# Earlier operand products and splits by DMA at the entry of a ConvFFN, on one core

## The chip, the cores and the metric

The kernel runs on one core of a Trainium2 chip. The metric is the device time of one execution in microseconds; lower is better. A core has the engines TensorE (PE in the profile, with its weight loads as PEld), VectorE (DVE), ScalarE (ACT), GpSimd (POOL) and SyncE (SP, which in this kernel issues the DMAs).

## The reference, cut to what matters

One decoder layer on 1024 tokens of 1024 channels, in float32: three token mixers, a merge, and then a pre-norm gated MLP with a causal convolution of width 3. The change lies where this MLP begins:

```python
x = x + merged @ w_o[l]

h = _rmsnorm(x, g_ffn[l])
u = _causal_dwconv(h @ w_up[l], ff_conv_w[l], ff_conv_b[l])
u_val, u_gate = jnp.split(u, 2, axis=-1)
x = x + (jax.nn.silu(u_gate) * u_val) @ w_down[l]
```

## The kernel before

Everything is held transposed: channels on the 128 partitions, tokens (reversed) along a row of 1024, in two halves of 512. A matrix product in float32 precision is made of three matmuls in the faster float32r format (`mm3`, lines 149 to 151). For this each operand is split in two: `hi` is the operand rounded to float32r, `lo` the rest. `split` writes `hi` on ACT (line 136) and `lo = src - hi` on DVE (line 137). Line 149 multiplies hi by hi, line 150 the weight's hi by the activation's lo, line 151 the weight's lo by the activation's hi. In the profile's names the tile after the arrow that comes first is the activation's part, the second the weight's (`whi`, `wlo`; both names serve for hi and lo of weights, since one tile holds both parts side by side).

Products with `w_up` go by a Strassen-Winograd scheme of seven half-size products. `seven` (from line 671) is a generator that makes one unit, that is two 128-column blocks of `w_up`, in four steps: step 1 the products with the operands `au` and `bu`, step 2 those with `t2` and `t3`, step 3 that with `t1`, step 4 those with `bl` and `t4`. For a unit it loads two weight tiles `r1` and `r2`, and DVE forms sums of their halves: `s1` (line 693), `a2 - ...` into the half `a2` (694), and `a1` for T2 (695). PSUM results are copied out by ACT (lines 689, 699, 704, 709) and added by DVE (691, 705, 712). Units 0, 1 and 2 (`first` in the code) are interleaved by hand at the entry. Their weight tiles are, by buffer number, raw_1423 and pg_1424 (unit 0), raw_1431 and pg_1432 (unit 1), me_1439, me_1440 and pg_1441 (unit 2).

The operands are linear combinations of the normalised halves. `bau` and `bbu` hold the upper half, ready before. At the entry, once `rows` is there (1/rms of the lower half's tokens, a PSUM tile ps_tr_1422 made by line 179), DVE forms the others for j = 0 and 1, each 128 x 1024: `diff[j]` (h_1301, h_1302) times `rows` is the source of t3; `full[j]` (pg_1289, pg_1290) plus `diff[j]` that of t2 (lines 1142 to 1148); `x1p[2+j]` (px_1351, px_1352) times gain and `rows` is bl, and bl minus `full[j]` is the source of t1, in `x1p[j]` (y_1349, y_1350; lines 1151 to 1157); `full[2+j]` (pg_1291, pg_1292) minus `full[j]` is that of t4 (lines 1160 to 1163). Their hi and lo parts are h_1398 to h_1401 (t2), pg_1402 to pg_1405 (t3), h_1406 to h_1409 (t1), pg_1410 to pg_1413 (bl) and h_1414 to h_1417 (t4); the lo parts have the odd numbers.

What sets the order: the code is traced as written, and a scheduler then gives each engine a fixed order by priority (the place in the code) and by what it estimates to be ready. `tc.high_priority(offset=n)` moves the instructions in its block forward in priority by n. Weight splits in `qring` have an offset of 40 (`SOON`). Each engine runs its own order strictly one after the other and waits at semaphores. DMAs are issued from SP's queue in its order; POOL issues none.

Of the kernel before, what the change touches and what calls it, by code (L numbers as in the profile page):

```python
# [10 lines left out]
F32 = mybir.dt.float32  # L11
F32R = mybir.dt.float32r
AF = mybir.ActivationFunctionType
ALU = mybir.AluOpType
# [28 lines left out]
def tile_hybrid_layer(ctx: ExitStack, tc: tile.TileContext, xT, memT, vecs, w_t, w_n, w_kv, w_if,  # L43
# [4 lines left out]
    nc = tc.nc  # L48
# [19 lines left out]
    def T(shape, tag, dt=F32, bufs=None):  # L68
        pool = {"mw": mlp, "mst": mlp, "px": late[0]}.get(tag, sb)
        return pool.tile(shape, dt, tag=tag, name=nm(tag), bufs=bufs or BUFS[tag])  # L70

    def page(tag="pg", dt=F32):
        return T([P, S], tag, dt)
# [4 lines left out]
    def wide():  # L78
        return T([P, S], "U")
# [22 lines left out]
    def hs(h):  # L102
        return slice(h * HALF, (h + 1) * HALF)
# [25 lines left out]
    def col(i, n=1):  # L129
        return vec[:, i:i + n]  # L130
# [4 lines left out]
    def split(src, hi, lo, eng=None):  # L135
        nc.scalar.activation(hi, src, AF.Copy)  # L136
        (eng or nc.vector).tensor_sub(lo, src, hi.bitcast(F32))  # L137

    def wsplit(src, tag=None, eng=None, raw=None):
        if raw is None:  # L140
            raw = T([P, S], "raw")
            nc.sync.dma_start(raw, src)
        hi = T([P, S], tag or "whi", F32R)
        lo = T([P, S], tag or "wlo", F32R)
        split(raw, hi, lo, eng)
        return hi, lo
# [21 lines left out]
    def rstd_rows(acc, n):  # L168

        return spread(rstd(acc, n), n // P)  # L170
# [111 lines left out]
    def x_norm(h, xp, rows):  # L282
        for j in range(4):
            t = wide()
            for k in (2 * j, 2 * j + 1):
                u = t[:, hs(k % 2)]
                nc.vector.scalar_tensor_tensor(u, xp[j][:, hs(k % 2)], col(C_GMIX + k), rows, op0=ALU.mult, op1=ALU.mult)  # L287
                split(u, hh[k][:, hs(h)], hl[k][:, hs(h)])
            nc.sync.dma_start(hn_d[h, j], t)
# [16 lines left out]
    for g in range(2):  # L306
        src = wraw[:, :, 4 * g:4 * g + 4]
        hi = wif[:, :, 32 * g:32 * g + 4]
# [352 lines left out]
    def qring(src):  # L661
        t = pair(turn(0, ("whi", "wlo")))
        with tc.high_priority(offset=SOON):
            split(src, *t)
        return t
# [399 lines left out]
    full = [page() for _ in range(4)]  # L1065
# [8 lines left out]
    diff = [page("h") for _ in range(2)]  # L1074
    for h in (1, 0):
        x1s = []
        acc = half()
        x1p = [wide() if h else T([P, S], ("y", "px")[i // 2]) for i in range(4)]
# [21 lines left out]
        for d in range(KT):  # L1100
            proj(w_o[d], m_hi, m_lo, ev(d), halves=(h,))
            if h == 0 and d > 0:
                if d == 1:
                    rows = rstd_rows(kept[0], HALF)
# [29 lines left out]
    fd, fx = {}, {"au": bau, "bu": bbu}  # L1134
# [3 lines left out]
    rows = rstd_rows(kept[0], HALF)  # L1138
    first = units[:3]
    for u in first:  # L1140
        next(u)
    for j in range(2):
        for i in range(2):
            nc.vector.tensor_mul(diff[j][:, hs(i)], diff[j][:, hs(i)], rows)
        nc.vector.tensor_add(full[j], full[j], diff[j])
        split(full[j], *fd["t2"][j])
    for j in range(2):
        split(diff[j], *fd["t3"][j])
    for u in first[:2]:
        next(u)  # L1150
    for j in range(2):
        bl = x1p[2 + j]
        for i in range(2):
            nc.vector.scalar_tensor_tensor(bl[:, hs(i)], bl[:, hs(i)], col(C_GFFN + 4 + 2 * j + i), rows,
                                           op0=ALU.mult, op1=ALU.mult)
        nc.vector.tensor_sub(x1p[j], bl, full[j])
        split(x1p[j], *fd["t1"][j])
    for u in first[:2]:
        next(u)
    for j in range(2):  # L1160
        split(x1p[2 + j], *fd["bl"][j])
        nc.vector.tensor_sub(full[2 + j], full[2 + j], full[j])
        split(full[2 + j], *fd["t4"][j])
    next(first[0])
    middle(first[2])
    next(first[1])
# [74 lines left out]
    au, al, bu, bl, wc = [], [], [], [], []  # L1241
# [167 lines left out]
```

## Time and profile before

| | us |
|---|---|
| three runs | 1677.52, 1679.14, 1679.28 (median 1679.14) |
| the profiled execution | 1682.24, span of the profile 1680.5 |
| PE busy | 1650.0 (98%) |
| DVE busy | 1209.4 (72%) |
| ACT busy | 825.4 (49%) |
| POOL busy | 51.7 (3%) |

All durations come from the one profiled execution; it took 3.1 us longer than the median of the three timed runs. The mean granted TensorE clock over it is 0.998 of full speed. The ConvFFN entry lies at 1040 to 1090 us of the span: line 1144 runs on DVE from 1046.4 to 1053.7, line 1154 from 1060.6, line 1156 from 1064.0, line 1162 from 1075.2. A row of a timeline gives start, length, engine, line, operation, out<-in and count, and in brackets how long the engine had been idle and who ended that. Rows of a DVE or ACT timeline overlap a little, since a length runs to the last write; how much an instruction holds its engine is read from one start to the next.

### The profile page before, as it was taken

The page shows a single profiled execution, that of the slowest core. Times are in us where ns is not written, and L with a number is a line of the kernel's source. Part 1 is how long each engine was busy: PE and PEld are TensorE (multiplying, and loading weights), DVE is VectorE, ACT ScalarE, POOL GpSimd, SP SyncE. Part 2 cuts the span into 40 slices and gives each one's busy share as a digit, 9 for nine tenths or more (in the row PEclk, how much of TensorE's full clock was granted, in tenths as well). Part 3 has the DMA queues.
Part 4 walks back from the last instruction along what each step waited for, and adds up shares of the span by engine and source line. Part 5 has one row for each costly group of instructions (what it writes and reads, how often), then busy time and mean ns, then how long its engine had stood idle before and what let it go on. Part 6 is the DMA issues. An engine that isn't in the chain of part 4 may idle for free.

```text
span 1680.5 us, 21196 instructions
## 1 busy us (share of the span) xinstructions
PE 1650.0 (98%) x7975; PEld 1340.4 (80%) x7975; DVE 1209.4 (72%) x1710; ACT 825.4 (49%) x1249; POOL 51.7 (3%) x95
## 2 busy tenths in 40 slices
PE   8999999999999999999999999999999999999999
PEld 4777777787777888888778888688888888788887
DVE  5648777777954766766457648997778877789864
ACT  4547677645544445656312334565555554543431
POOL 1000000010000101000000000000000000000000
PEclk9999999999999999999999999999999999999999
DMA  8421011233334564422856354222222221486142
GB/s 294 148 64 33 26 39 51 98 122 114 122 117 150 189 185 151 142 101 102 283 180 192 108 190 149 83 93 100 88 76 75 76 89 62 163 325 238 33 139 74
DMA packets 96249, 212.69 MB, mean 127 GB/s; under 512 B 12416, under 2 KB 36224, under 8 KB 96148
## 3 DMA queue, kind: packets, MB, share of 16 engines
q1 hardware_dynamic: 96148, 211.35, 37.0%
q8 instruction: 63, 1.03, 0.3%
q14 instruction: 38, 0.31, 0.1%
HBM read 156.71 MB, written 54.61 MB: 126 GB/s over the span
## 4 chain that ended last, share of the span: by engine, by line
PE 88%; DVE 4%; ACT 4%; DMA 3%; issue 1%; SPq 0%; POOLq 0%; ACTq 0%; DVEq 0%
PE ps_pj L149 14%; PE ps_pj L150 14%; PE ps_pj L151 14%; PE ps_pv L150 6%; PE ps_pv L149 6%; PE ps_pv L151 6%; PE ps_tr L149 4%; PE ps_tr L151 4%; PE ps_tr L150 4%; PE ps_z L149 3%; PE ps_z L150 3%; PE ps_z L151 2%; PE ps_tr L434 2%; PE ps_pv L448 1%; PE ps_z L226 1%
## 5 line engine op out<-in xcount | busy, mean ns | idle before, releaser
L150 PE MATMUL ps_pj<-h,whi 128*128 128x512 f32 x620 | 242.5, 391 | 0.0
L136 ACT ACTIVATE whi<-raw 128x512 fp32r<-128x512 f32 (+1 forms) x112 | 93.6, 836 | 181.1 <-PE ps_pj L150 75.8
L149 PE MATMUL ps_pj<-h,whi 128*128 128x512 f32 x412 | 163.3, 396 | 1.3 <-DVE U L1052 1.2
L149 PE MATMUL ps_pj<-pg,whi 128*128 128x512 f32 x396 | 155.4, 393 | 0.7 <-ACT U L699 0.7
L151 PE MATMUL ps_pj<-pg,wlo 128*128 128x512 f32 x380 | 148.2, 390 | 0.2 <-DVE wlo L137 0.2
L150 PEld LDWEIGHTS ps_pj<-h,whi 128*128 128x128 f32 x620 | 116.5, 188 | 23.6 <-DVE U L287 0.2
L151 PE MATMUL ps_pj<-h,wlo 128*128 128x512 f32 x332 | 130.1, 392 | 0.7 <-DVE wlo L137 0.7
L810 DVE SCALAR_TENSOR_TENSOR y<-U,vec,y 128x1023 f32<-128x1023 f32 x88 | 112.4, 1279 | 8.0 <-ACT y L808 8.0
L422 DVE TENSOR_TENSOR_SCAN U<-U 128x512 f32<-128x512 f32 (+3 forms) x96 | 88.6, 965 | 30.6 <-ACT U L415 29.7
L149 PEld LDWEIGHTS ps_pj<-h,whi 128*128 128x128 f32 x412 | 77.5, 188 | 18.6 <-ACT whi L136 1.6
L137 DVE TENSOR_TENSOR wlo<-raw,whi 128x1024 fp32r<-128x1024 f32 x54 | 66.0, 1222 | 33.4 <-ACT whi L136 33.4
L149 PEld LDWEIGHTS ps_pj<-pg,whi 128*128 128x128 f32 x396 | 74.5, 188 | 16.9 <-ACT U L699 1.6
L151 PEld LDWEIGHTS ps_pj<-pg,wlo 128*128 128x128 f32 x380 | 71.4, 188 | 15.5 <-DVE wlo L137 0.6
L136 ACT ACTIVATE whi<-pg 128x512 fp32r<-128x512 f32 (+1 forms) x59 | 43.4, 738 | 73.5 <-PE ps_pv L150 20.3
L151 PEld LDWEIGHTS ps_pj<-h,wlo 128*128 128x128 f32 x332 | 62.4, 188 | 14.3 <-DVE wlo L137 1.6
L150 PE MATMUL ps_pj<-pg,whi 128*128 128x512 f32 x188 | 73.7, 392 | 0.0
L150 PE MATMUL ps_pv<-h,whi 128*128 128x512 f32 x164 | 63.9, 390 | 0.0
L808 ACT ACTIVATE y<-U,vec 128x1024 f32<-128x1024 f32 x44 | 54.6, 1241 | 15.2 <-DVE U L712 15.2
L151 PE MATMUL ps_pj<-h,whi 128*128 128x512 f32 x156 | 60.9, 390 | 0.0
L151 PE MATMUL ps_tr<-pg,wlo 128*128 128x512 f32 x144 | 56.2, 390 | 0.3 <-DVE wlo L137 0.3
L137 DVE TENSOR_TENSOR whi<-raw,whi 128x512 fp32r<-128x512 f32 x58 | 39.9, 688 | 23.0 <-ACT whi L136 22.7
L436 ACT ACTIVATE y<-ps_tr 128x1024 f32<-128x1024 f32 (+3 forms) x48 | 39.1, 814 | 31.6 <-PE ps_tr L434 31.2
(438 smaller groups left out, 4314.3 us busy)
## 6 DMA issues: line engine op xcount, KB each, us to landing
raw<-in_w_t_dram SPq DMA_DIRECT2D x29, 512.0 KB, 3.8
gate_d<-U SPq DMA_DIRECT2D x24, 512.0 KB, 3.0
U<-gate_d SPq DMA_DIRECT2D x24, 512.0 KB, 3.9
pg<-in_w_up_dram SPq DMA_DIRECT2D x22, 512.0 KB, 3.9
act_d<-y SPq DMA_DIRECT2D x22, 512.0 KB
pg<-in_w_t_dram SPq DMA_DIRECT2D x21, 512.0 KB, 4.6
raw<-in_w_dn_dram SPq DMA_DIRECT2D x18, 512.0 KB, 3.4
raw<-in_w_o_dram SPq DMA_DIRECT2D x16, 512.0 KB, 3.4
```

Source lines behind the costliest of these rows:

```text
L136: nc.scalar.activation(hi, src, AF.Copy)
L137: (eng or nc.vector).tensor_sub(lo, src, hi.bitcast(F32))
L149: nc.tensor.matmul(out, lh, rh, start=start, stop=False, skip_group_check=more)
L150: nc.tensor.matmul(out, lh, rl, start=False, stop=False, skip_group_check=more)
L151: nc.tensor.matmul(out, ll, rh, start=False, stop=stop, skip_group_check=more)
L226: nc.tensor.matmul(pm[m], mg[k // 4][:, c], w[:, hs(kk)], start=(k == 0), stop=(k == KT - 1))
L422: nc.vector.tensor_tensor_scan(f[:, a, 1:w + 1], f[:, a, 1:w + 1], f[:, a, 1:w + 1], 1.0 if o == 0 else f[:, a, 0:1], op0=ALU.mult, op1=AL ...
L434: nc.tensor.transpose(pt[:, a, ts(j)], g[:, a, ts(j)], ident)
L436: nc.scalar.activation(wt[:, :, :w], pt[:, :, :w], AF.Copy)
L448: nc.tensor.matmul(pv[64 * a:64 * a + 64, ts(rb % 4)], sbv[s // 2][:, s % 2, (2 * p + a) * 64:(2 * p + a + 1) * 64], wt[:, a, ts(j)], star ...
L808: nc.scalar.activation(out, u, AF.Identity, bias=bias, scale=taps[0])
L810: nc.vector.scalar_tensor_tensor(out[:, :S - s], u[:, s:], taps[s], out[:, :S - s], op0=ALU.mult, op1=ALU.add)
```

## The change

A new helper, `split_add`, writes `hi` on ACT, then `-hi` on ACT into the tile of `lo`, and then adds the source to it by a DMA that GpSimd issues. It is used for the six tiles of t1, bl and t4. The lines that form t2 and t3, with their splits, get a priority offset of 200.

```diff
+    def split_add(src, hi, lo):
+
+        nc.scalar.activation(hi, src, AF.Copy)
+        nc.scalar.activation(lo, hi.bitcast(F32), AF.Copy, scale=-1.0)
+        nc.gpsimd.dma_start(lo, src, accum_op=ALU.add)
...
-    for j in range(2):
-        for i in range(2):
-            nc.vector.tensor_mul(diff[j][:, hs(i)], diff[j][:, hs(i)], rows)
-        nc.vector.tensor_add(full[j], full[j], diff[j])
-        split(full[j], *fd["t2"][j])
-    for j in range(2):
-        split(diff[j], *fd["t3"][j])
+    with tc.high_priority(offset=200):
+        for j in range(2):
+            for i in range(2):
+                nc.vector.tensor_mul(diff[j][:, hs(i)], diff[j][:, hs(i)], rows)
+            nc.vector.tensor_add(full[j], full[j], diff[j])
+            split(full[j], *fd["t2"][j])
+        for j in range(2):
+            split(diff[j], *fd["t3"][j])
...
-        split(x1p[j], *fd["t1"][j])
+        split_add(x1p[j], *fd["t1"][j])
...
-        split(x1p[2 + j], *fd["bl"][j])
+        split_add(x1p[2 + j], *fd["bl"][j])
         nc.vector.tensor_sub(full[2 + j], full[2 + j], full[j])
-        split(full[2 + j], *fd["t4"][j])
+        split_add(full[2 + j], *fd["t4"][j])
```

Lines behind the helper move down by six, and those behind the new block by seven (L695 becomes L701, L704 becomes L710, L1154 becomes L1161).

The order on DVE right behind the first two L693 rows (units 0 and 1), before:

```order
L694 TENSOR_TENSOR pg_1424_8632<-raw_1423_8630,pg_1424_8632 128x512
L694 TENSOR_TENSOR pg_1432_8675<-raw_1431_8673,pg_1432_8675 128x512
L695 TENSOR_TENSOR raw_1423_8630<-hf_1430_8669,raw_1423_8630 128x512
L695 TENSOR_TENSOR raw_1431_8673<-hf_1438_8712,raw_1431_8673 128x512
L693 TENSOR_TENSOR hf_1447_8757<-pg_1441_8720 128x512
L1144 TENSOR_TENSOR h_1301_7943<-h_1301_7943,ps_tr_1422_8628 128x512
```

and in the changed kernel, where the first of these rows stands too, from the row behind it (the L1151 rows are L1144 of before, L1152 is L1145, L700 and L701 are L694 and L695):

```order
L1151 TENSOR_TENSOR h_1301_7943<-h_1301_7943,ps_tr_1422_8628 128x512 x2
L1151 TENSOR_TENSOR h_1302_7944<-h_1302_7944,ps_tr_1422_8628 128x512
L1152 TENSOR_TENSOR pg_1289_7931<-pg_1289_7931,h_1301_7943 128x1024
L1151 TENSOR_TENSOR h_1302_7944<-h_1302_7944,ps_tr_1422_8628 128x512
L137 TENSOR_TENSOR pg_1403_8599<-h_1301_7943,pg_1402_8598 128x1024
L137 TENSOR_TENSOR h_1399_8595<-pg_1289_7931,h_1398_8594 128x1024
L1152 TENSOR_TENSOR pg_1290_7932<-pg_1290_7932,h_1302_7944 128x1024
L137 TENSOR_TENSOR pg_1405_8601<-h_1302_7944,pg_1404_8600 128x1024
L137 TENSOR_TENSOR wlo_1444_8724<-me_1439_8716,wlo_1444_8724 128x512
L137 TENSOR_TENSOR h_1401_8597<-pg_1290_7932,h_1400_8596 128x1024
L697 TENSOR_TENSOR U_1428_8651<-U_1428_8651,ps_z_1426_8635 128x512
L701 TENSOR_TENSOR raw_1423_8630<-hf_1430_8669,raw_1423_8630 128x512
```

The ten rows that form and split t2 and t3 now stand ahead of the sum that makes raw_1423, the T2 weight of unit 0.

The order on ACT from the hi part of t1, before (U_1449 and U_1453 are results of units 0 and 1 copied from PSUM):

```order
L136 ACTIVATE h_1406_8602<-y_1349_8246 128x1024
L136 ACTIVATE h_1408_8604<-y_1350_8247 128x1024
L689 ACTIVATE U_1445_8739<-ps_tr_1442_8722 128x512
L699 ACTIVATE U_1449_8790<-ps_tr_1425_8634 128x512
L136 ACTIVATE wlo_1456_8851<-hf_1430_8669 128x512
L699 ACTIVATE U_1453_8823<-ps_pj_1433_8677 128x512
L136 ACTIVATE wlo_1458_8897<-raw_1423_8630 128x512
L704 ACTIVATE U_1449_8790<-ps_tr_1425_8634 128x512
```

and in the changed kernel, from the row before the second hi part (L142 writes -hi, L695, L705 and L710 are L689, L699 and L704 of before):

```order
L142 ACTIVATE h_1407_8603<-h_1406_8602 128x1024
L141 ACTIVATE h_1408_8604<-y_1350_8247 128x1024
L695 ACTIVATE U_1445_8739<-ps_tr_1442_8722 128x512
L705 ACTIVATE U_1449_8790<-ps_tr_1425_8634 128x512
L705 ACTIVATE U_1453_8823<-ps_pj_1433_8677 128x512
L142 ACTIVATE h_1409_8605<-h_1408_8604 128x1024
L136 ACTIVATE wlo_1458_8903<-raw_1423_8630 128x512
L136 ACTIVATE whi_1460_8923<-pg_1424_8632 128x512
L142 ACTIVATE pg_1411_8607<-pg_1410_8606 128x1024
L141 ACTIVATE h_1414_8610<-pg_1291_7933 128x1024
L141 ACTIVATE pg_1412_8608<-px_1352_8249 128x1024
L142 ACTIVATE h_1415_8611<-h_1414_8610 128x1024
```

The next two rows there are `L710 ACTIVATE U_1449` and then the pass that writes -hi of the second bl tile, pg_1413: the new passes stand between and behind copies that wait for PE.

POOL's queue had no DMA; in the changed kernel it ends with these six, in this order:

```order
L143 DMA h_1407_8603<-y_1349_8246 128x1024
L143 DMA h_1409_8605<-y_1350_8247 128x1024
L143 DMA pg_1411_8607<-px_1351_8248 128x1024
L143 DMA h_1415_8611<-pg_1291_7933 128x1024
L143 DMA pg_1413_8609<-px_1352_8249 128x1024
L143 DMA h_1417_8613<-pg_1292_7934 128x1024
```

Each waits for ACT's -hi pass of its tile, and the matmuls of line 150 with that tile (L156 now) wait for its landing.

On PE, the 60 matmuls from the first with t3 or t2 (number 4179 in its order) to the last ahead of t1 (4238) are the same set in another order; those with t1, bl and t4 (from 4239) keep their place within a few rows.

## The prediction

> **What bounds the kernel now.** I read the page's head first, then the chain that ended last, then a table of stretches around the changed place, and last the timeline of each engine there.
>
> ```profile
> span 1680.5 us, 21196 instructions
> ...
> PE 1650.0 (98%) x7975; PEld 1340.4 (80%) x7975; DVE 1209.4 (72%) x1710; ACT 825.4 (49%) x1249; POOL 51.7 (3%) x95
> ...
> PE 88%; DVE 4%; ACT 4%; DMA 3%; issue 1%; SPq 0%; POOLq 0%; ACTq 0%; DVEq 0%
> ```
>
> TensorE (PE) is the bound: any microsecond that it stands still is a microsecond of the span, and work taken off VectorE (DVE) or ScalarE (ACT) is worth something only where PE waits for it. So the question is how long PE waits at the ConvFFN entry now. The table of stretches (length, busy time by engine, granted clock, DMA share, GB/s) answers that:
>
> ```profile
> core 0: us, PE busy (x) PEld busy (x) DVE busy (x) ACT busy (x) POOL busy (x), PEclk, DMA share, GB/s
> ...
> 1052.00:1056.00 4.00, 1.71 (x5) 0.93 (x5) 4.00 (x6) 3.58 (x4) 0.00 (x0) 0.94 0.00 0
> 1056.00:1060.00 4.00, 4.00 (x13) 3.12 (x13) 4.00 (x5) 1.06 (x1) 0.00 (x0) 0.63 0.00 0
> 1060.00:1064.00 4.00, 4.00 (x19) 3.34 (x18) 2.57 (x5) 1.28 (x2) 0.00 (x0) 1.00 0.00 0
> 1064.00:1071.00 7.00, 6.74 (x28) 4.74 (x27) 7.00 (x10) 3.96 (x6) 0.00 (x0) 1.00 0.00 0
> 1071.00:1073.00 2.00, 0.99 (x5) 0.60 (x5) 2.00 (x4) 2.00 (x5) 0.00 (x0) 1.00 0.00 0
> 1073.00:1100.00 27.00, 27.00 (x119) 21.92 (x118) 26.66 (x34) 16.75 (x24) 0.00 (x0) 1.00 0.50 172
> ```
>
> PE is idle 2.3 of the 4 us from 1052, then runs 4 us at a clock of 0.63, which loses 0.37 x 4.00 = 1.5 us (a "dip" below); it is idle 0.26 us before 1071 and 1.0 us after it. From 1073 on it is never idle: 119 matmuls in 27.00 us, 0.227 us each. The whole prize is thus about 2.3 + 1.5 + 0.3 + 1.0 = 5.1 us, 0.3% of the span. About 0.2% (3.4 us) is what a measurement of this kernel can tell from no change. PE's timeline places the waits (start, length, line, tiles, and in brackets the idle time and who ended it):
>
> ```profile
> 1051.65 0.39 PE L151 MATMUL ps_z<-h,whi 128*128 128x512 f32 x1
> 1053.75 0.50 PE L149 MATMUL ps_pv<-pg,whi 128*128 128x512 f32 x1 [1.72 <-ACT pg L136]
> ...
> 1056.15 0.63 PE L151 MATMUL ps_pv<-pg,whi 128*128 128x512 f32 x1
> ...
> 1065.87 0.50 PE L151 MATMUL ps_pj<-h,wlo 128*128 128x512 f32 x1 [0.26 <-DVE wlo L137]
> ...
> 1072.16 0.50 PE L149 MATMUL ps_tr<-h,wlo 128*128 128x512 f32 x1 [1.01 <-ACT wlo L136]
> 1072.50 0.40 PE L150 MATMUL ps_tr<-h,wlo 128*128 128x512 f32 x1
> ```
>
> In PE's order the row at 1056.15 is the fifth matmul with the new operands t2 and t3 (number 4183), and the one at 1072.50 is the first that reads a lo part of t1 (number 4240). These numbers hold in both kernels, and I compare at them.
>
> **Part 1: the higher priority of t2 and t3.** The split operands come earlier on DVE, and the weight sums of units 0 and 1 (L694, L695) come later. The T2 product needs both.
>
> ```profile
> 1043.34 1.29 DVE L694 TENSOR_TENSOR pg<-raw,pg 128x512 f32<-128x512 f32 x2
> 1044.54 1.29 DVE L695 TENSOR_TENSOR raw<-hf,raw 128x512 f32<-128x512 f32 x2
> ...
> 1052.55 1.22 DVE L1145 TENSOR_TENSOR pg<-pg,h 128x1024 f32<-128x1024 f32 x1
> 1053.68 0.68 DVE L1144 TENSOR_TENSOR h<-h,ps_tr 128x512 f32<-128x512 f32 x1
> ...
> 1065.73 1.40 DVE L1154 SCALAR_TENSOR_TENSOR px<-px,vec,ps_tr 128x512 f32<-128x512 f32 x2
> 1067.05 1.22 DVE L137 TENSOR_TENSOR h<-y,h 128x1024 fp32r<-128x1024 f32 x1
> ```
>
> A 512-wide DVE row takes 1.20 / 2 = 0.60 us of the engine, a 1024-wide one 1.13. Unit 0's sum raw_1423 was started at 1044.54. Now it stands after the first L694 row (1043.34 + 0.60 = 1043.94) and after four 512-wide products, two 1024-wide sums, four 1024-wide lo splits and two other 512-wide rows; with its own 0.60 that is 7 x 0.60 + 6 x 1.13 = 11.0, so it ends at 1055.0. Its hi split on ACT and its lo split on DVE follow. ACT's rows:
>
> ```profile
> 1047.68 0.63 ACT L136 ACTIVATE wlo<-raw 128x512 fp32r<-128x512 f32 x1
> ...
> 1065.53 1.04 ACT L136 ACTIVATE h<-y 128x1024 fp32r<-128x1024 f32 x1
> ...
> 1071.00 0.59 ACT L699 ACTIVATE U<-ps_tr 128x512 f32<-128x512 f32 x1
> 1071.48 0.63 ACT L136 ACTIVATE wlo<-hf 128x512 fp32r<-128x512 f32 x1
> ```
>
> The hi split (0.63) lets PE go on at 1055.7; the lo split stands two DVE rows further (start 1056.1) and frees number 4183 at 1056.85, where before it started at 1056.15: 0.7 us later. What was waited for (operand splits) is early; what was early (the weight) is late. PE's gap becomes about 3.6 us in one piece instead of several, and I leave the dip of 1.5 us that follows as it is (bounds: none, or twice that). From there to number 4240 are 57 matmuls, 12.9 us. The waits of before at 1065.87 and 1072.16 go: the weight splits that ended them (wlo_1452 on DVE, wlo_1456 on ACT) stand earlier in the new orders. PE arrives at 1056.85 + 12.9 + 1.5 = 1071.3 instead of 1072.5: part 1 gains 1.2 us, if t1 is there.
>
> **Part 2: lo parts by DMA.** Six 1024-wide DVE subtracts go (6.8 us of DVE, hidden under PE's 27.00 of 27.00 us after 1073, so worth nothing there); six ACT passes of 1.04 us come, and six DMAs of 512 KB on POOL's queue, SBUF to SBUF, adding. Call T the time from the end of the ACT pass to the landing. The trace has no accumulating DMA, none on POOL and none from SBUF to SBUF. The nearest rows (KB, median us from issue to landing, and POOL's smallest arithmetic):
>
> ```profile
> pg<-in_xT_dram SPq DMA_DIRECT2D x8, 512.0 KB, 8.1
> hn_d<-U SPq DMA_DIRECT2D x8, 512.0 KB, 2.6
> ...
> hf<-in_xT_dram SPq DMA_DIRECT2D x16, 256.0 KB, 2.6
> px<-in_w_up_dram SPq DMA_DIRECT2D x8, 512.0 KB, 3.3
> ...
> L157 POOL TENSOR_TENSOR sm<-sm,nhalf 128x4 f32<-128x4 f32 (+2 forms) x19 | 25.1, 1320 | 490.2 <-DVE sm L155 455.3 <-ACT hf L136 34.9
> ```
>
> Two loads, 256 KB in 2.6 and 512 KB in 3.3 us, give 0.7 us per 256 KB and 1.9 fixed. An accumulating DMA reads the operand and the destination, 1024 KB: 1.9 + 4 x 0.7 = 4.7; with POOL's 1.3 us to start even a 4-column operation, T = 6.0 by estimate. The low end is the fastest 512 KB row, 2.6, with an issue of 0.3: T = 2.9; nothing that moves the same bytes was faster. The high end is the slowest group above, 8.1, plus 1.3: T = 9.4. I take 6.0, between the ends and nearest to the unloaded weight loads, since DMA share was 0.00 when the first of the six would run.
>
> t1[0]: on DVE, y_1349 stands eight 512-wide rows and three L1154 rows (1065.73 to 1067.05 for two, 0.66 each) after 1056.1 in the new order, hence starts at about 1062.9 and ends at 1064.1. ACT: hi 1.04, one weight split 0.5, -hi 1.04, so the DMA can be issued at 1066.75, and lands at 1066.75 + T. PE asks at 1071.3: it waits T - 4.55 = **1.45 us**. (The DVE subtract of before started at 1067.05 and was done at 1068.3.)
>
> t1[1]: its -hi stands on ACT behind three PSUM copies (0.5 each), the first of which waits for the end of PE's number 4229 (46 matmuls and the dip after 4183: about 1069.2). So it ends at 1071.7, 4.95 us after that of t1[0], while PE has only 13 matmuls, 2.95 us, between the two: it waits another **2.0 us** for any T over 4.55 (T - 2.55 below that).
>
> bl[1]: here the added ACT pass is queued behind a wait. pg_1413's -hi follows the copy U_1449 (L704 before), which waits for the last T1 matmul of unit 0 (number 4257). From that matmul's start: 0.39 + 0.5 + 1.04 = 1.95 us to the issue, then T; PE needs it at 4281, 24 matmuls or 5.45 us on: it waits T - 3.5 = **2.5 us**. Before, DVE did this lo in time. The second t4 part is late by 0.1 at most, and I leave it out.
>
> On SP, a load of the next unit's weights takes over px_1351's buffer:
>
> ```profile
> 1075.33 0.33 SPq L680 DMA_DIRECT2D px<-in_w_up_dram  x1
> ```
>
> It now waits for the DMA that reads this buffer, until about 1080, and the loads behind it on SP wait too; PE needs them 66 matmuls (15 us) after 4281, and such a load lands in 3.3 us, so that costs nothing. DVE's later rows follow PE and have slack.
>
> Dips: three waits of 1.45, 2.0 and 2.5 us within some 12 us look like the 2.3 us idle in 4 that brought the clock of 0.63, so I add two dips, one for the t1 pair, one for bl[1]: 2 x 1.5 = 3.0 us (bounds: 0 and three, 4.5). The Trainium skill, TensorE: Matmul & The Clock Gate, Part 1, says that the clock is halved only after an idle window of about 3.4 us and comes back after as long a busy one. The trace gave its dip after 2.3 us of idle in 4, so it does not quite agree; by that rule these three waits bring no dip and the sum is 3.0 us less.
>
> Sum at T = 6.0: -1.2 + 1.45 + 2.0 + 2.5 + 3.0 = **+7.75 us**. The profiled execution took 1682.24 us (span 1680.5), 3.1 us over the median of 1679.14; the difference is the same against either, so the forecast is 1679.14 + 7.75 = **1687 us**, 0.46% slower.
>
> **Rivals.** (a) The DMA is hidden, the other side: not slower. It decides at T = 4.5: there t1[0] costs 0, t1[1] 2.0, bl[1] 1.0 and at most one dip 1.5, less 1.2: +3.3, just under 0.2%. At T = 2.9 only t1[1] costs, 0.35: 0.35 - 1.2 = -0.85, 1678.3 us. For it speaks the 2.6 us store; against it that two operands must be read, and that POOL starts nothing in under a microsecond of arithmetic. Even without the first dip too (-1.5) it is 2.4 us faster, which nobody could tell from no change. By the Trainium skill, DMA: Bandwidth & Descriptors, Anatomy of one DMA, a DMA from GpSimd takes about 2.0 us plus its bytes at 436 GB/s, which for 512 KB would be an estimated 3.2 us: this rival. No run here shows a DMA of that kind.
>
> (b) The DMA is slow. The bl and t4 DMAs fall where SP's weight loads already held a DMA share of 0.50, and they share one queue. At T = 9.4: 4.85 + 2.0 + 5.9 + 4.5 - 1.2 = +16, 1695 us. It decides from T = 8. Against it: the t1 DMAs at least have the engines to themselves.
>
> **How the numbers follow.** Forecast (T from 4.5 to 8) 0.56, slow DMA 0.20, hidden DMA 0.24. The first two are slower by over 0.2%: 0.76. Of the hidden case I give 0.18 to within 0.2% and 0.06 to faster, for a saving that these rows do not show. The range, 1679 to 1697, takes in most of (a) and (b) with its upper bound; the forecast's own range is 1682.5 to 1693.
>
> **What would show it.** In the changed kernel's profile: the first T2 matmul waits for ACT's split of raw at about 1055.7; the first matmul with t1's lo waits for a DMA on POOL's queue, then again for the second, then one with bl's; DMA issues on POOL land in about 5 us; granted clock under 1 around 1056 and again after 1072. It is wrong if those DMAs land within 3 us of their issue, if PE is not idle for them, or if the T2 wait is over 2 us longer than worked out.

## The result, and the profile after

| | before | changed |
|---|---|---|
| median of six runs each, us | 1678.33 (1677.19 to 1682.55) | 1689.11 (1687.81 to 1693.34) |
| ratio of times | | 1.0053, interval 1.004 to 1.0066 |
| profiled execution, us | 1682.24 (span 1680.5) | 1693.34 (span 1691.6) |
| PE, DVE, ACT, POOL busy, us | 1650.0, 1209.4, 825.4, 51.7 | 1655.0, 1203.2, 832.1, 57.7 |

The measured ratio puts the loss at 8.9 us (6.7 to 11.1); the two medians lie 10.8 us apart, which is inside that interval. The profiled execution of the changed kernel is the slowest of its six, 4.2 us over their median, so its single times are held against a second profile of the same kernel (e9) further down. Where the loss lies is seen by a stage time: from PE's eight small matmuls of the norm (L165 before, L171 in the changed kernel), which lie ahead of all that is changed, to the fifth Silu pass on ACT, from where the units follow each other every 19.04 us in both kernels. In the timeline of before (start, length, engine, line, operation):

```profile
1038.67 0.98 PE L165 MATMUL ps_tr<-ones,hf 128*128 128x1 f32 x8
...
1152.60 1.06 ACT L1123 ACTIVATE y<-y 128x1024 f32<-128x1024 f32 x1 [0.25 <-DVE y L810]
```

and of the changed kernel:

```profile
1039.56 0.98 PE L171 MATMUL ps_tr<-ones,hf 128*128 128x1 f32 x8
...
1164.14 1.06 ACT L1129 ACTIVATE y<-y 128x1024 f32<-128x1024 f32 x1 [0.26 <-DVE y L816]
```

The stage took 113.93 us before and takes 124.58 now, 10.65 more, against 11.1 more in the whole profiled execution: the whole loss lies here. The changed kernel's times are 0.89 us later at the first row; I take that off where a time is compared with one of before (e9's first row stands 1.32 us earlier than that of before, and there I add as much).

PE's timeline in the changed kernel, its idle times in brackets:

```profile
1056.69 0.80 PE L155 MATMUL ps_tr<-h,wlo 128*128 128x512 f32 x1 [3.29 <-ACT wlo L136]
...
1063.00 0.39 PE L156 MATMUL ps_pv<-pg,whi 128*128 128x512 f32 x1
...
1074.49 0.50 PE L156 MATMUL ps_tr<-h,wlo 128*128 128x512 f32 x1 [1.12 <-DMA h<-y]
...
1079.78 0.64 PE L156 MATMUL ps_tr<-h,wlo 128*128 128x512 f32 x1 [2.03 <-DMA h<-y]
...
1090.27 0.80 PE L156 MATMUL ps_tr<-pg,wlo 128*128 128x512 f32 x1 [2.22 <-DMA pg<-px]
...
1096.72 0.50 PE L156 MATMUL ps_pv<-h,whi 128*128 128x512 f32 x1 [1.19 <-DMA h<-pg]
```

The first is the gap ahead of T2, which waits for the weight split of raw_1423. The other four wait for DMAs that write lo parts: t1 twice, bl and t4, 1.12 + 2.03 + 2.22 + 1.19 = 6.56 us. The stretches behind them (PE, PEld, DVE, ACT, POOL busy with counts, granted clock, DMA share, GB/s):

```profile
1056.00:1060.00 4.00, 3.31 (x7) 2.32 (x8) 4.00 (x7) 1.26 (x2) 0.00 (x0) 0.51 0.00 0
1060.00:1064.00 4.00, 4.00 (x13) 3.14 (x12) 2.83 (x6) 0.63 (x1) 0.00 (x0) 0.64 0.00 0
1064.00:1068.00 4.00, 4.00 (x20) 3.30 (x19) 4.00 (x6) 2.84 (x4) 0.00 (x0) 1.00 0.00 0
...
1076.00:1080.00 4.00, 1.97 (x9) 1.33 (x8) 0.00 (x0) 2.61 (x3) 1.74 (x2) 1.00 0.99 196
1080.00:1084.00 4.00, 4.00 (x12) 3.12 (x12) 0.69 (x1) 1.59 (x3) 0.00 (x0) 0.58 1.08 232
...
1092.00:1096.00 4.00, 3.53 (x12) 2.46 (x11) 2.29 (x3) 2.88 (x4) 0.00 (x0) 0.80 0.91 244
```

The clock falls behind the gap and behind the waits of 2.03 and 2.22, not behind those of 1.12 and 1.19. From 1056.69 to 1063.00 there are 14 matmul starts, which at full clock take 14 x 0.227 = 3.18 us: the front dip cost 3.1 us. In the same way (start to start, less 0.227 each, where the clock is low) the other two cost 1.7 each; before, the one dip cost 1.8. The DMA issues of GpSimd, with KB and the median time from issue to landing:

```profile
h<-y POOLq DMA_DIRECT2D x2, 512.0 KB, 5.2
pg<-px POOLq DMA_DIRECT2D x2, 512.0 KB, 6.8
h<-pg POOLq DMA_DIRECT2D x2, 512.0 KB, 8.0
```

In ACT's timeline, the pass that makes -hi of bl's second part (L142) stands right behind the copy (L710) that had waited for PE:

```profile
1082.17 0.60 ACT L710 ACTIVATE U<-ps_tr 128x512 f32<-128x512 f32 x1 [3.55 <-PE ps_tr L157]
1082.66 1.05 ACT L142 ACTIVATE pg<-pg 128x1024 fp32r<-128x1024 f32 x1
```

### The profile page after: what moved, and what is told of

Its sections match the earlier page's. It is cut to its first block, busy times and chain, and to the rows that moved or that the text cites. A ratio compares the mean times of both kernels' runs of the same rounds, so it can differ in the third digit from the quotient of the medians.

```text
span 1691.6 us, 21221 instructions
## 1 busy us (share of the span) xinstructions
PE 1655.0 (98%) x7975; PEld 1343.3 (79%) x7975; DVE 1203.2 (71%) x1704; ACT 832.1 (49%) x1255; POOL 57.7 (3%) x101
## 3 DMA queue, kind: packets, MB, share of 16 engines
q1 hardware_dynamic: 96148, 211.35, 36.5%
q0 software_dynamic: 864, 3.15, 1.0%
## 4 chain that ended last, share of the span: by engine, by line
PE 86%; DVE 4%; DMA 4%; ACT 4%; issue 1%; SPq 0%; POOL 0%; ACTq 0%; DVEq 0%; POOLq 0%
PE ps_pj L156 13%; PE ps_pj L155 13%; PE ps_pj L157 13%; PE ps_pv L157 6%; PE ps_pv L156 6%; PE ps_pv L155 6%; PE ps_tr L157 4%; PE ps_tr L155 4%; PE ps_tr L156 4%; PE ps_z L155 3%; PE ps_z L156 2%; PE ps_z L157 2%; PE ps_tr L440 1%; PE ps_pv L454 1%; PE ps_z L232 1%
## 5 line engine op out<-in xcount | busy, mean ns | idle before, releaser
L156 PE MATMUL ps_pj<-h,whi 128*128 128x512 f32 x620 | 242.5, 391 | 0.0
L156 PEld LDWEIGHTS ps_pj<-h,whi 128*128 128x128 f32 x620 | 116.8, 188 | 23.7 <-issue 0.2
L156 PE MATMUL ps_pj<-pg,whi 128*128 128x512 f32 x188 | 73.6, 392 | 0.0
L156 PE MATMUL ps_pv<-h,whi 128*128 128x512 f32 x164 | 64.0, 390 | 1.2 <-DMA h<-pg 1.2
L137 DVE TENSOR_TENSOR whi<-raw,whi 128x512 fp32r<-128x512 f32 x58 | 39.9, 688 | 23.4 <-ACT whi L136 23.3
```

Source lines behind the costliest of these rows:

```text
L156: nc.tensor.matmul(out, lh, rl, start=False, stop=False, skip_group_check=more)
```

## The experiments

Theory A, the prediction's: the time is lost in PE's waits for the adding DMAs and in the dips behind the longer ones, while the priority change gains a little. Rivals: the priority change is the loss (B), or the second ACT pass (C). The table has what all runs gave. "Stage" is the difference from 113.93 us; "idle" the sum of PE's idle times from the norm's L185 (L179) row to 1130 us, without those under 0.2 us that the timeline does not list; "dips" the time lost to a lower clock, worked out as above. The ratios are of times against before on the same chip. "Filled" are matmuls by zero.

| kernel | ratio (95%) | stage, us | idle, us | dips, us |
|---|---|---|---|---|
| before | 1 | 0 | 3.9 | 1.8 |
| changed | 1.0053 (1.004 to 1.0066) | +10.65 | 10.3 | 6.5 |
| e1 priority only | 0.9991 (0.9982 to 1.0) | -1.30 | 4.1 | 1.8 |
| e2 DMAs only | 1.0055 (1.0042 to 1.0068) | +9.08 | 10.2 | 3.5 |
| e3 -hi pass, added by DVE | 0.9999 (0.999 to 1.0008) | +0.11 | 5.1 | 1.5 |
| e4 waits filled | 1.0061 (1.0048 to 1.0074) | +10.28 | 9.2, and 4.8 filled | 1.8 |
| e5 plain copies | 1.0029 (1.0016 to 1.0042) | +2.90 | 6.7 | 1.8 |
| e6 DMAs for t4 only | 1.0025 (1.0016 to 1.0034) | +3.69 | 7.2 | 3.5 |
| e7 priority, gap filled | 0.999 (0.9981 to 0.9999) | -1.32 | 1.6, and 3.2 filled | 0 |
| e8 weight sums first | 0.9995 (0.9986 to 1.0004) | -1.62 | 3.2 | 0 |
| e9 changed again | 1.0063 (1.0051 to 1.0075) | +9.52 | 11.8 | 3.2 |
| e10 half DMAs | 1.0075 (1.0063 to 1.0087) | +11.57 | 12.0 | 4.5 |
| e11 priority, GpSimd subtracts | 1.0026 (1.0016 to 1.0037) | +3.01 | 6.5 | 2.9 |
| e12 bl early on ACT | 1.0076 (1.0062 to 1.0089) | +12.64 | 12.7 | 6.1 |

Idle, dips and filled time, less the 5.7 us of before, explain each stage to within 1.6 us, and to within 0.8 us in the kernels with both parts of the change (changed, e4, e5, e9, e10, e12; for the changed kernel 16.8 - 5.7 = 11.1 against 10.65). Differences of about 1 us between the fast kernels (e1, e3, e7, e8) are therefore not explained by these columns.

**One part alone: e1 and e2.** e1 calls the old `split` in the three places; e2 leaves out the priority.

```diff
# e1
-        split_add(x1p[j], *fd["t1"][j])
+        split(x1p[j], *fd["t1"][j])
...
# e2
-    with tc.high_priority(offset=200):
+    if True:
```

> Only the priority change: the lo parts of t1, bl and t4 by VectorE's subtract as before. Theory A (the time is lost in PE's waits for the adding DMAs, and in the clock dips behind the longer ones): the four waits of 1.12, 2.03, 2.22 and 1.19 us are gone; the front gap of about 3.3 us and the dip of about 3.4 us behind it stay, but they cost what the scattered waits and the dip of before cost, so 1677 to 1681 us, within 0.2% of before. Theory B (the priority change loses the time: one idle of 3.3 us in place of several, with a dip of 3.4 us): slower than before by 4 us or more, 1682 to 1689. Theory C (the added ScalarE passes lose it): as A.

> Only the six adding DMAs: the priority block is taken out. Theory A: waits for the DMAs of t1 and t4 or bl of 1 to 3 us each, about 6.5 us in all, and two dips of 1.7 us: slower than before by 8 to 13 us, 1686 to 1692. Theory B: the loss goes with the priority, so at most 3 us slower than before, 1678 to 1682. Theory C: as A, 1686 to 1692.

PE's waits in e1 (in all, count, longest), from 1037 to 1104 us:

```profile
PE ps_tr L155 <- ACT wlo L136: 3.3, 1, 3.3
PE ps_tr L185 <- DVE hf L183: 0.5, 1, 0.5
PE ps_tr L157 <- DVE wlo L137: 0.3, 1, 0.3
```

and in e2:

```profile
PE ps_tr L156 <- DMA h<-y: 3.2, 1, 3.2
...
PE ps_pv L156 <- DMA h<-pg: 1.7, 2, 1.4
...
PE ps_tr L156 <- DMA pg<-px: 1.3, 1, 1.3
```

Both as theory A has it: without the DMAs the gap of 3.3 us stays and the kernel is no slower (0.09% faster by its ratio, with an interval that reaches 1.0); with the DMAs alone it is as slow as the changed kernel. B falls.

**The second ACT pass: e3.** VectorE adds the operand to -hi in place of the DMA.

```diff
-        nc.gpsimd.dma_start(lo, src, accum_op=ALU.add)
+        nc.vector.tensor_add(lo, src, lo.bitcast(F32))
```

> The changed kernel, but VectorE adds the operand to -hi in place of the DMA; ScalarE's second pass stays. Theory A: no wait for a DMA; PE waits for ScalarE's later splits and copies by 0.2 to 1.2 us at two or three places, none of them long enough for a dip: 1 to 4 us slower than before, 1679.5 to 1682.5. Theory C: ScalarE's six passes of about 1.0 us are what delays PE, so nearly all of the loss stays: 8 to 11 us slower than before, 1686 to 1690. Theory B: as C, since the priority block is in.

The stage is 1.4 us longer than e1's, with two new waits of 0.65 and 0.41 us for ACT, and the time is that of before (-1.7 to +1.3 us, under the 1 to 4 that I expected). Theory C falls: the DMA itself is what costs.

**The dips: e4 and e7.** A helper adds matmuls by a tile of zeros to a running sum: in e4 ten in unit 0's T1 and eleven in its bl sum ahead of the waiting matmul, in e7 (on e1) fourteen ahead of T2.

```diff
+    def fill(p, rhs, n):
+        for _ in range(n):
+            nc.tensor.matmul(p, zr, rhs, start=False, stop=False, skip_group_check=True)
```

> The changed kernel with 10 matmuls by zero weights (0.227 us each) in unit 0's T1 sum and 11 in its bl sum, put just ahead of the matmul that waits for the second t1 part and for the second bl part: they add zero, and keep PE busy where it would be idle. The DMAs land when they did. If theory A is right in that the clock dips come from PE's idle: the two dips of about 1.7 us behind 1079.8 and 1090.3 go, the granted clock stays 1.00 there, and the time is 2 to 4 us under the changed kernel's 1689.1: 1685 to 1687.5. If the lower clock there has another cause (the DMA traffic): no gain, 1689 to 1691.

> The priority change alone, with 14 matmuls by zero weights (3.18 us) put into the front gap ahead of the first T2 matmul, which adds zero to unit 0's sum. If the dip behind that gap comes from PE's idle: the gap of 3.3 us becomes one of 0.1 to 0.3 us, the granted clock stays 1.00 from 1052 to 1066, and the 1.5 to 1.9 us of the dip are gained less up to 1 us that PE waits later: 1.5 to 3.5 us under before. If the dip has another cause: the same as the priority change alone, 1.5 us under before.

In e4 PE's timeline shows the ten at the second t1 part, and what is left of the wait:

```profile
1073.18 2.49 PE L681 MATMUL ps_tr<-h,zr 128*128 128x512 f32 x10
1077.03 0.50 PE L688 MATMUL ps_tr<-h,wlo 128*128 128x512 f32 x1 [0.66 <-DMA h<-y]
```

and its stretches there:

```profile
1080.00:1084.00 4.00, 3.80 (x17) 2.81 (x16) 1.98 (x3) 2.62 (x5) 0.87 (x1) 1.00 1.07 212
...
1088.00:1092.00 4.00, 1.93 (x9) 1.29 (x8) 0.44 (x1) 1.98 (x3) 0.00 (x0) 1.00 1.04 333
```

The clock stays at 1.00 while the DMA share is over 1 (the times of packets overlap there): idle, not traffic, brings the dips. In e7 it stays at 1.00 too, and the gap of 3.3 us is gone. But neither is faster. In e4 the waits fell by 1.4 us (6.56 to 5.19) and two dips by 3.4, which is just the 4.8 us of the filling: the filled matmuls did not only stand where PE was idle, they went ahead of other units' matmuls that PE had done before the wait. In e7 the filling's 3.2 us took the place of the gap's 3.3, a new wait of 0.8 us for ACT came behind, and the dip of 1.8 was saved; the gain left by that, 1 us, is less than the intervals of e1 and e7 can tell, and the stage does not show it. So it is shown that the dips come from PE's idle; that they can be avoided at no cost is not.

**What makes the landing late: e5, e6 and e10.** e5 drops the addition, all else in place; e6 uses the DMA for t4 alone; e10 does each operand in halves.

```diff
# e5
-        nc.gpsimd.dma_start(lo, src, accum_op=ALU.add)
+        nc.gpsimd.dma_start(lo, src)
...
# e10
+        for i in range(2):
+            nc.scalar.activation(hi[:, hs(i)], src[:, hs(i)], AF.Copy)
+            nc.scalar.activation(lo[:, hs(i)], hi[:, hs(i)].bitcast(F32), AF.Copy, scale=-1.0)
+            nc.gpsimd.dma_start(lo[:, hs(i)], src[:, hs(i)], accum_op=ALU.add)
```

> The changed kernel with the six DMAs as plain copies: the operand is written over -hi and not added to it, so the lo parts are wrong and the subtraction is left out; every instruction, its engine and its order are the same. It tells whether the adding makes the landing late. Theory D1 (adding is what is slow: it must read its destination too): landings of 2.6 to 3.5 us after the issue, where the adding ones took 5.2 to 8.0; the waits of 1.12, 2.03, 2.22 and 1.19 us shrink to under 1 us each, no dip behind them, and the time is within 3 us of the kernel before. Theory D2 (the size, the queue of GpSimd or the path from SBUF to SBUF is what is slow): landings stay above 4.5 us, and the time is 6 to 11 us over before, as the changed kernel's.

> The priority change, and adding DMAs for the t4 operand alone; t1 and bl by VectorE's subtract. If each DMA's wait costs by itself (theory A): one or two waits of 0.1 to 2.5 us at the first t4 matmuls and at most one dip of 1.5 to 1.9 us, so 0 to 4 us over the kernel with the priority change alone, that is -1.5 to +2.5 us against before. If the DMAs were slow only because six stood in one queue (theory Q): no wait for t4 at all, and the time of the kernel with the priority change alone, 1.5 us under before. The second t4 DMA landed 8.0 us after its issue in the changed kernel; alone in the queue it should take about 5 us by theory Q, about 7 or more if SyncE's weight loads are what slows it.

> The changed kernel with each operand's hi pass, -hi pass and adding DMA done in two halves of 512 columns: twelve DMAs of 256 KB. Landings so far: 3.2 us for a plain 512 KB copy, 5.2 for an adding one, so 2.0 us for each 512 KB that is moved and 1.2 fixed. If the bytes set the landing (theory D1): a half lands about 3.2 us after its issue, PE can start on the first half, the waits of 1.1 to 2.2 us shrink to under 1.2 us each, no dip behind them: 1 to 5 us over before. If a fixed cost of each DMA sets it (theory D3: GpSimd's 0.87 to 1.08 us per issue and the start of the DMA): halves land no sooner than 4.5 us, twelve issues delay the last ones, and the time is 7 us or more over before.

The DMA issues in e5, to be held against the three rows of the changed kernel above:

```profile
q0 software_dynamic: 864, 3.15, 0.5%
...
h<-y POOLq DMA_DIRECT2D x2, 512.0 KB, 3.2
pg<-px POOLq DMA_DIRECT2D x2, 512.0 KB, 4.5
h<-pg POOLq DMA_DIRECT2D x2, 512.0 KB, 4.3
```

Without the addition a landing is 2.0 to 3.7 us earlier, and the waits shrink to 1.0, 1.2 and 0.5 us. D1's figure of 2.6 to 3.5 us holds for t1 alone: bl's and t4's plain copies still take 4.5 and 4.3 us, so adding is not all that is slow there. For the time, too, D1 went too far, since by the ratio 4.9 us (2.7 to 7.1) of the loss stay where I had said at most 3 (the stage of the profiled execution is 2.9 longer). The plain copies, too, come after the second ACT pass and through GpSimd's queue.

In e6 one wait for a DMA is left, longer than any of those in the changed kernel's first profile:

```profile
1082.25 0.50 PE L156 MATMUL ps_pv<-h,whi 128*128 128x512 f32 x1 [3.10 <-DMA h<-pg]
```

and the stretch ahead of it has the engines busy with SyncE's loads as well:

```profile
1076.00:1080.00 4.00, 3.15 (x14) 2.26 (x13) 3.93 (x6) 3.66 (x6) 0.72 (x2) 1.00 0.93 224
```

It is for t4's first part. The two landings took 6.6 and 5.0 us: alone in GpSimd's queue they are faster than the 8.0 of six, but not fast enough. Two of the six DMAs cost 5.7 us over e1 (0.34%), about half of the whole; theory Q falls, and theory A's bound of 4 us was too low. So the waits of single DMAs do not add up: in the changed kernel PE's waits for t1 and bl give t4's DMAs time. That SyncE's loads slow the landings is read from the DMA share beside them (0.93 here, up to 1.08 in the changed kernel); no run took the loads away, so it is argued and not shown.

e10's halves:

```profile
h<-y POOLq DMA_DIRECT2D x4, 256.0 KB, 3.9
pg<-px POOLq DMA_DIRECT2D x4, 256.0 KB, 6.5
h<-pg POOLq DMA_DIRECT2D x4, 256.0 KB, 7.7
```

Half the bytes save 1.3 us for t1 and 0.3 for the others, and the kernel is not faster: its median is 2.7 us over that of e9 on the same chip, with intervals that overlap. Neither theory fits as written: t1's first tile came earlier (PE waited 0.34 us for it, where it had waited 1.12), but for its second PE waited 0.21 + 2.10 us, no less than the 2.03 for a whole tile, and the later halves came as late as whole tiles.

**The order ahead of the gap, and the dip's length: e8 and e9.** e8 is before, with the weight sums of units 0 and 1 in a priority block of 60; e9 is the changed kernel once more.

```diff
-        nc.vector.tensor_add(s1, a2, b2)
-        nc.vector.tensor_sub(a2, a1, a2)
-        nc.vector.tensor_sub(a1, s1, a1)
+        with tc.high_priority(offset=OFF[0]):
+            nc.vector.tensor_add(s1, a2, b2)
+            nc.vector.tensor_sub(a2, a1, a2)
+            nc.vector.tensor_sub(a1, s1, a1)
```

> The kernel before, with the other side of the choice at the front: the weight sums of the first two units get a priority of 60, and the products, splits and lo parts stay as they were. The idle of 1.72 us at 1053.75 should fall into pieces of at most 1.3 us. If pieces that short bring no dip: 1.5 to 2.5 us under before; if the dip comes from the sum of idle in a few microseconds: within 0.1% of before.

> The changed kernel once more, beside the two below on one chip: 0.4 to 0.7% slower than before by every theory, with PE waits for the adding DMAs of 1.1, 2.0, 2.2 and 1.2 us. Open is the dip behind the front gap of 3.3 us: it was 3.1 us in the first profile of this kernel and 1.5 to 1.8 us in four other kernels with the same gap. If its length depends only on the gap, it is 3.1 us again; if on when the gap falls, 1.5 to 1.9 us here.

e8's waits:

```profile
PE ps_tr L149 <- ACT wlo L136: 1.0, 1, 1.0
PE ps_pv L150 <- DVE pg L137: 0.9, 1, 0.9
PE ps_tr L150 <- DVE h L137: 0.8, 1, 0.8
```

No idle of over 1.0 us, and a clock of 1.00 in every stretch from 1048 to 1072. The stage is 1.6 us shorter; the time (0.8 us less, between 2.4 less and 0.7 more) cannot be told from before. e9's front dip cost 1.5 us where the first profile's had cost 3.1, behind the same gap of 3.29 us: its length depends on when the gap falls.

The clock in the traces shows how. It is either 1.00 or 0.50, and it changes only at points that lie whole multiples of 3.41 us apart: in the changed kernel it is 0.50 from 1056.09 to 1062.91, from 1079.98 to 1083.39 and from 1090.22 to 1093.63, and 1079.98 - 1056.09 = 23.89 is 7 times 3.413. Cut into these pieces, the two profiles of the changed kernel give (PE idle is the piece less PE's busy time in it):

| profile | piece, us | PE idle in it, us | clock in it | clock in the next |
|---|---|---|---|---|
| changed | 1052.67 to 1056.09 | 2.68 | 1.00 | 0.50 |
| changed | 1056.09 to 1059.50 | 0.60 | 0.50 | 0.50 |
| changed | 1059.50 to 1062.91 | 0 | 0.50 | 1.00 |
| changed | 1076.57 to 1079.98 | 2.03 | 1.00 | 0.50 |
| e9 | 1051.51 to 1054.92 | 2.98 | 1.00 | 0.50 |
| e9 | 1054.92 to 1058.34 | 0.20 | 0.50 | 1.00 |
| e9 | 1071.99 to 1075.40 | 0.99 | 1.00 | 1.00 |
| e9 | 1075.40 to 1078.82 | 1.04 | 1.00 | 1.00 |

The front gap reached 0.60 us into the slow piece in the first profile, and the clock stayed low for another piece; in e9 only 0.20 us were idle there, and it came back. The wait of 2.03 us for t1's second part lay in one piece and brought a dip; the same wait, 2.04 us in e9, was cut in two by the edge of a piece and brought none. Where the edges fall differs from one execution to the next: the front dip starts 16.5 us behind the norm's row in the first profile and 17.6 us in e9. Over the fourteen profiles, between 1045 and 1100 us, a full-speed piece with 2.03 us or more of idle was followed by a slow one all 18 times, one with 1.64 or less never, but for one of 1.40 us in e2; a slow piece with 0.43 us or more of idle was followed by another (6 times), one with 0.29 or less by full speed (19 times). In e7 and e8, which have no slow piece there, the edges are counted back from the slow piece at the end of the span.

e9's waits for bl:

```profile
PE ps_tr L156 <- DMA pg<-px: 4.7, 2, 3.8
```

4.7 us where the first profile had 2.22 for bl and 1.19 for t4: the later landings vary from run to run. Counted from the norm's row, bl's second DMA was issued 2.1 us earlier than in the first profile and landed no earlier (50.9 against 50.7 us behind that row).

**The front by GpSimd, and ACT's order: e11 and e12.** e11 (on e1) gives three of the front's subtracts to GpSimd; e12 gives bl's split in the changed kernel a priority of 100.

```diff
# e11
+            split(full[j], *fd["t2"][j], nc.gpsimd if j in (1,) else None)
...
+            split(diff[j], *fd["t3"][j], nc.gpsimd if j in (0, 1) else None)
# e12
+        with tc.high_priority(offset=100):
+            split_add(x1p[2 + j], *fd["bl"][j])
```

> The priority change, with ordinary lo parts, but three of the front's four 1024-wide subtracts (the second t2 part and both t3 parts) on GpSimd: VectorE's queue ahead of the weight sum raw_1423 is 3 x 1.13 = 3.4 us shorter, which is the length of the front gap. If GpSimd takes up to about 2.5 us for such a subtract and does not hold up VectorE: the gap of 3.3 us and its dip of 1.8 us go, the time is 4 to 6 us under before (0.25 to 0.35%). If GpSimd takes 4 us or more, or VectorE is slowed while it works: PE waits for the t2 and t3 lo parts instead, and the time is no better than with the priority change alone, -1.5 us or worse.

> The changed kernel with a priority of 100 for bl's hi pass, -hi pass and adding DMA: on ScalarE both bl parts' -hi now stand ahead of the copy U_1449 that waits for unit 0's last T1 matmul, where the second stood behind it; but the second t1 part's -hi stands behind two more 1024-wide passes (0.95 us each). If ScalarE's queue sets the wait for bl's second part (2.2 us in the changed kernel's first profile, 3.8 in its second): that wait is at most 0.5 us here, the wait for the second t1 part grows by 1 to 2.5 us from its 2.0, and the time is 8 to 13 us over before: a wait moved, not saved. If the landing alone sets it: PE still waits 1.5 us or more for bl's second part.

GpSimd's two subtracts in a row, and its single one, in e11's timeline:

```profile
1047.54 5.63 POOL L137 TENSOR_TENSOR pg<-h,pg 128x1024 fp32r<-128x1024 f32 x2 [5.08 <-ACT pg L136]
1055.42 2.36 POOL L137 TENSOR_TENSOR h<-pg,h 128x1024 fp32r<-128x1024 f32 x1 [2.26 <-ACT h L136]
```

VectorE's at the same time:

```profile
1046.88 1.22 DVE L1152 TENSOR_TENSOR pg<-pg,h 128x1024 f32<-128x1024 f32 x1
...
1050.84 3.42 DVE L1152 TENSOR_TENSOR pg<-pg,h 128x1024 f32<-128x1024 f32 x1
...
1055.91 2.42 DVE L701 TENSOR_TENSOR raw<-hf,raw 128x512 f32<-128x512 f32 x1
```

GpSimd takes 2.4 us for the single subtract, as hoped, and 2.7 to 2.8 for each of the two in a row, but the same L1152 addition on VectorE takes 3.42 us beside it where it took 1.22 ahead of it, and the weight sum raw_1423 takes 2.42, where the next one took 0.68. It ends no earlier, and PE is idle 2.74 and 2.45 us: slower than e1, the second case of the expectation. GpSimd's second subtract ends at 1047.54 + 5.63 = 1053.17, the addition at 1050.84 + 3.42 = 1054.26, 1.1 us later, which is its own length. In the same way GpSimd's single subtract ends at 1057.78 and the weight sum at 1058.33, 0.55 us later: VectorE did not run slower, it stood still until GpSimd was done.

e12's waits for DMAs are now all for t1:

```profile
PE ps_tr L156 <- DMA h<-y: 7.6, 2, 6.5
```

PE no longer waits for bl. It comes there later than in the changed kernel, but that alone is not the reason: counted from the norm's row, bl's second DMA was issued 5.0 us earlier and landed 2.5 us earlier (8.7 us after its issue, where the first profile had 6.2), more than the 2.22 us of the wait. So ACT's order had set that wait; for a PE as early as in e9 about 1.1 us of its 3.8 would be left by these rows. The second t1 part, whose -hi stands behind two more passes and whose DMA stands behind bl's, costs 6.5 us, not the 3 to 4.5 I had put: a wait was moved, and made larger.

No kernel tried beats before by more than 0.1%; e1 and e7 are the best, and their intervals end at 1.0 and 0.9999.

## Why the prediction was right, and where its sum was off

The forecast was 1687 us, 7.75 over before; measured were 8.9 us (6.7 to 11.1) in the first comparison and 10.6 (8.6 to 12.6) in e9. The direction and the mechanism hold; the sum is short by 1 to 3 us. In the prediction's own terms the first profile gives 0 (part 1) + 1.12 + 2.03 (t1) + 2.22 (bl) + 1.19 (t4) + 3.4 (dips) = 10.0 us of the stage's 10.65, and e9 gives -1.1 + 1.11 + 2.04 + 4.69 + 0 + 1.7 = 8.4 of 9.52; the forecast was -1.2 + 1.45 + 2.0 + 2.5 + 0 + 3.0.

- **Part 1** (gains 1.2 us): held. The first T2 matmul was to start at 1055.7, behind a gap of 3.6 us, and starts at 1056.69 - 0.89 = 1055.80, behind 3.29. The first matmul with t1's lo was to be reached at 1071.3; in e9, whose norm row stands 1.32 us earlier than that of before, it starts at 1071.16 after a wait of 1.11, so it was reached at 1070.05 + 1.32 = 1071.37. The dip of 1.5 that was taken over was 1.5 to 1.8 in seven of the eight other profiles with the gap of 3.3 us; in e12 it was 3.2 and in the changed kernel's first 3.1, so that part 1 gained nothing in that one execution.
- **T = 6.0**: from the end of the ACT pass to the matmul that waited for the landing it was 5.1 us for t1's first part, 6.0 for its second, 6.6 for bl's second (1082.66 + 1.05 to 1090.27) and 9.2 for t4's second. The value was near for the first three and close to the upper bound of 9.4 for the last. In e9 it was 5.1 and 6.0 for t1 again, but 8.9 for bl's second part (1078.40 + 1.05 to 1088.30).
- **t1[0], 1.45 us**: 1.12. Three sizes were off and nearly cancel: the issue came 1.7 us later than worked out, the landing took 0.9 less, and PE, held up by the longer front dip, came 1.2 later. **t1[1], 2.0 us**: 2.03. **bl[1], 2.5 us**: 2.22; in e9 3.81, and 0.88 more for bl's first part, which the sum had not late at all. That the first profile came so near is partly luck. The queueing of bl[1]'s -hi behind the copy U_1449 is what the ACT rows above show, and e12 shows what it is worth by moving it.
- **The step that failed is one T for all six DMAs, and with it "t4[1] late by 0.1 at most".** PE waited 1.19 us for it in the first profile and not at all in e9, where it had waited the longer for bl; in e6, where t4 alone goes by DMA, it waited 3.1 for t4's first part. The later DMAs had a T of 6.6 to 9.2, not 6.0. The prediction's own rival (b) had named what may make them slower: from 1080 us on SyncE's weight loads and GpSimd's DMAs together held a DMA share of up to 1.08.
- **Two dips, 3.0 us**: 1.7 + 1.7 in the first profile, a single one of 1.7 in e9. How many come is decided by where the waits fall among the pieces of 3.41 us, which the rows of before do not tell; that there were two in the first profile is luck. The rule of the Trainium skill (TensorE: Matmul & The Clock Gate, Part 1), by which there would have been none, asks for an idle window of about 3.4 us; here waits of 2.03 and 2.22 us brought one each, while 2.04 in e9 and 2.08 in e4, each cut in two by an edge, brought none. The same page of the Trainium skill says that the window runs freely, and the traces agree: the edges lie 3.41 us apart, and the same gap of 3.29 us cost 1.5 us in one profile and 3.1 in another. They differ from the page in that a piece need not be idle as a whole: 2.03 us of idle in 3.41 were enough.
- **ACT's six passes at nothing**: e3 against e1 gives 1.4 us of the stage, within the intervals of the times. This may be part of the shortfall; it is not resolved.
- **The weight load into px_1351's buffer, at nothing**: it was issued 7.3 us later than before (1083.51 - 0.89 against 1075.33), and no wait of PE for a load appears up to 1130 us.
- **Rival (a), the hidden DMA**: by the Trainium skill (DMA: Bandwidth & Descriptors, Anatomy of one DMA) 512 KB from GpSimd land in an estimated 3.2 us. e5's plain copies of t1 landed in just 3.2; the adding ones took 5.2. The rule holds for the copy with the engines free (those of bl and t4 took 4.5 and 4.3), and an addition is not one. The prediction had reasoned that two operands must be read; the runs show that an addition holds the engines for about twice the time, which fits that reason without proving it.

## What to carry to other kernels

Cost a transfer that adds to its destination as about two transfers, on engines that other loads share, and count it from the end of the pass that prepares it. For 512 KB that was 5.1 us for the first, ahead of all other transfers, and 6.0 to 9.2 for those beside others, so it hides only where the result has that much time to spare, not where the next matmul wants it. Taking work from an engine that has slack (VectorE was under PE's cover here) buys nothing, and the replacement's latency is then the whole price. A wait that is taken off one operand by priority can come back at the next operand in the same queue, as in e12: work out who is late next before moving it. Do not read one profile's clock dips as the kernel's own: the same wait brought a dip in one execution and none in the next.

## What the runs showed of the hardware

- An adding DMA keeps the engines busy for about twice the time of a copy of the same size: the six moved 3.15 MB in 1.0% of 16 engines' span in the changed kernel and in 0.5% in e5. By the first share that is 3.15 MB / (0.010 x 1691.6 us x 16) = 11.6 GB/s for each engine, by the second (0.005 x 1682.6 us x 16) 23.4; the other queue's 211.35 MB in 36.5% go at 21.4.
- A half-size adding DMA is not half as long: 3.9 against 5.2 us for t1, 6.5 and 7.7 against 6.8 and 8.0 for bl and t4, beside loads (medians, from issue to landing).
- PE's clock is settled anew every 3.41 us, at edges that do not follow the kernel (16.5 and 17.6 us behind the same row in two executions): it was 1.00 or 0.50 for a whole piece, and low for 3.41, 6.83 or (e12) 10.24 us. Nearly always it fell behind a piece with 2.03 us or more of PE idle and stayed up behind one with 1.64 or less (one of 1.40 in e2 is the exception); from low it came back only behind a piece with 0.29 us of idle or less. So a single wait of 1.72 us brought a dip in before, together with another of 0.43 in the same piece, and single waits of 2.04 (e9), 2.08 (e4) and 2.10 us (e10) brought none, because an edge cut them.
- A GpSimd subtract from SBUF holds up VectorE's operations on two SBUF operands until it is done (3.42 against 1.22 us). The Trainium skill says so (SBUF — State Buffer, Who interferes with whom: with two SBUF inputs VectorE contends with a GpSimd instruction that reads SBUF, and the second one blocks); I had left it open, and e11 agrees with the page.
